# Moving the last third of a mixer's output projection into the next layer's tiles

## The chip, the cores and the metric

One core of a Trainium2 chip. The metric is the device time of one execution in microseconds (us), median over runs. Before the change it is 3393.17 us (three runs, 3390.63 to 3396.44).

## The reference

An encoder block over a sample of 1024 tokens and a prompt of 512 tokens, 1024 features, in fp32. Each of three layers has the same frame: normalise, compute, normalise the result, add it to the input.

```python
def rmsnorm(x, g):
    return x * lax.rsqrt(jnp.mean(x * x, axis=-1, keepdims=True) + NORM_EPS) * g
def swiglu(h, w1, w3, w2):
    return (jax.nn.silu(h @ w1) * (h @ w3)) @ w2
```

The order is: a half-step feed-forward (`ffn1`, hidden width 2816), the mixer (an input projection, a hyena long convolution on half of the channels, a two-way retention on the other half, an output projection with `w_out`, 1024 by 1024), and a second half-step feed-forward (`ffn2`). "Layer 1" below is `ffn1`, "layer 2" is `ffn2`.

## The kernel before, in words

**Layout.** Features lie on the 128 partitions and tokens along the columns, 1536 of them (1024 of the sample, then 512 of the prompt). An fp32 product is made of three TensorE passes: every operand is split in a high part (`hi_act`, L59, a copy on ScalarE) and a low part (`lo`, L62, a subtraction on VectorE or GpSimd), and `mm3` issues high-high (L67), high-low (L68) and low-high (L69). So a weight tile needs a load, a copy and a subtraction before its matmuls.

**Feed-forward.** `ffn` (L424) takes the columns in two halves, g = 0 (columns 0 to 767) and g = 1 (768 to 1535). Its up products (`up_unit`, tiles `ua`, `ub`, `uc`, 128x384) work on seven combinations of quarter blocks, `b11`, `b21`, `b22`, `t1` to `t4`, which `operands` (L241) builds and splits from the normalised input `xq` (`normed`, L215 to 233, which multiplies by the row of reciprocal norms `rq`). `down` (L336) makes the second product (tile `dn`), `post_quads` (L399) closes it: sums of squares (`ss`, L205), reciprocal roots (`rstd`, L86 to 100, one of its steps, L95, on GpSimd), spread over the partitions on TensorE (`rps`, L212), multiply, add the input, store. Work for the next half runs `beside` the units, a step at a time.

**Mixer, input side.** `norm_T` (L155) loads a segment of 512 columns of layer 1's output, multiplies it by the reciprocal norms (L169) and splits it into `hh` (ScalarE) and `hl` (GpSimd, L62). Then `w_in_v` (tile `v`, weights split into `w2h` and `w2l`) and `w_in_pass` (tile `wips`) multiply it by the input weights.

**Mixer, output side.** `out_proj(g)` (L1121) takes three thirds of 512 columns. `load_y` loads and splits the mixer's result into `yh` and `yl`. `proj` (L498) walks over eight output blocks of 128 features, each 8 x 3 = 24 matmuls of 128x512 (tile `proj`); the weights are loaded at L506 and their low part is made on GpSimd. `post` (L520) collects each block: its squares on ScalarE (L531), its product with the gain on VectorE (L532), the sum of squares on VectorE (L534). After the eighth block it closes the third: column sums (`rstd_cols`, `ssc`, L126), reciprocal roots, `rps` (L130), eight products z * rps (L546), eight additions of the mixer's input `o` (L547, alternately on VectorE and GpSimd), the store to `x2`, and for thirds 0 and 1 the reciprocal norms for layer 2 (`rstd_rows`).

Layer 2's first half needs columns 0 to 767, hence the closings of thirds 0 and 1; its second half needs third 2 as well.

**Order.** Every DMA is issued by SyncE. A planner simulates the program as written and fixes one order for each engine; the engines then run in that order and wait on semaphores. Tiles come from pools with a fixed number of places: a tile waits until the place that it gets is released.

Of the kernel before, what the change touches and what calls it, by code (L numbers as in the profile page):

```python
# [15 lines left out]
D = 1024  # L16
# [30 lines left out]
class Kern:  # L47
# [55 lines left out]
    def rstd_rows(self, acc, psp, rp, tag, row, **kw):  # L103


        nc = self.nc
        hl = self.xp.tile([128, 2, 512], F32R, tag="x", name="sqs")
        hi, lo = hl[:, 0], hl[:, 1]
        self.hi_act(hi, acc)
        self.lo(nc.vector, lo, acc, hi)  # L110
        ss = psp.tile([128, 512], F32, tag="nr", name="ss")
        nc.tensor.matmul(ss, lhsT=self.ones, rhs=hi, start=True, stop=False)
        nc.tensor.matmul(ss, lhsT=self.ones, rhs=lo, start=False, stop=True)
        out = rp.tile([128, 512], F32, tag=tag, name="rrow", **kw)
        nc.scalar.activation(out[0:1], ss[0:1], AF.Copy)
        c = self.sp.tile([128, 8], F32, tag="nc", name="nc")[:, :4]
        nc.sync.dma_start(c, out[0:1].rearrange("o (p c) -> o p c", c=4))
        r = self.rstd(c, 1.0 / D)
        nc.sync.dma_start(row.rearrange("o (p c) -> (o p) c", c=4), r)

    def rstd_cols(self, acc, psp, half):

        nc = self.nc
        ss = psp.tile([128, 512], F32, tag="nr", name="ssc")[:, :4]
        for t in range(4):
            nc.tensor.matmul(ss[:, t:t + 1], lhsT=acc[:, t * 128:(t + 1) * 128], rhs=self.one, start=True, stop=True)  # L126
        r = self.rstd(ss, 1.0 / D, half)
        ps = psp.tile([128, 512], F32, tag="nr", name="rps")
        for t in range(4):
            nc.tensor.transpose(ps[:, t * 128:(t + 1) * 128], r[:, t:t + 1].broadcast_to([128, 128]), self.ident)  # L130
        return ps

# [11 lines left out]

    def add_sq(self, acc, x, out, first):

        nc = self.nc
        nc.scalar.activation(out, x, AF.Square)
        if first:
            nc.vector.tensor_tensor(acc, out[:, 0], out[:, 1], ALU.add)  # L150
        else:
            for j in range(2):
                nc.vector.tensor_tensor(acc, out[:, j], acc, ALU.add)
# [24 lines left out]

    def bank(self, name):
        return self.pm.tile([128, 512], F32, tag="mm", name=name)[:, :384]  # L180
# [60 lines left out]
    def operands(self, load, X, Y):  # L241
# [17 lines left out]
        b["t3"] = self.split(Y, h12, "t3")  # L259
        b["t1"] = self.split(Y, t1, "t1")  # L260
        b["t4"] = self.split(Y, t2, "t4")
# [162 lines left out]
    def ffn(self, n, srcs, dsts, row_in, row_out, Y, side):  # L424
# [21 lines left out]
        with pool("xq", 6, side=side) as X, pool("fs", side=side) as self.fs, pool("ft", 6, side=side) as self.ft, \  # L446
                pool("fw", 10, side=side) as self.fw, pool("fr", 5, side=side) as self.fr, pool("pm", 8, space=PSUM) as self.pm:
            h = [], []
            for th in range(2):
                for _ in ready(0, th, h[th]):  # L450
                    pass
            for _ in self.operands(lambda kh, th: h[th][kh], X, Y):
                pass

            def ahead():

                for th in range(2):
# [40 lines left out]
    def proj(self, aT, w, nk, psd, wp, rp, done, eng):  # L498


        nc = self.nc
        ah, al = aT
        nb = w.shape[2]
        for c in range(w.shape[0]):
            raw = rp.tile([128, nb, 128], F32, tag="raw", name="raw2")
            nc.sync.dma_start(raw, w[c])  # L506
            for i in range(0, nb, KD):
                wh = wp.tile([128, KD, 128], F32R, tag="w", name="w2h")
                wl = wp.tile([128, KD, 128], F32R, tag="w", name="w2l")
                self.hi_act(wh, raw[:, i:i + KD])  # L510
                self.lo(eng[(i // KD + c) % len(eng)], wl, raw[:, i:i + KD], wh)
                for j in range(KD):
                    m, k = divmod(c * nb + i + j, nk)
                    if k == 0:
                        ps = psd.tile([128, 512], F32, tag="mm", name="proj")
                    self.mm3(ps, wh[:, j], wl[:, j], ah[k], al[k], k == 0, k == nk - 1)
                    if k == nk - 1:
                        done(m, ps)

    def post(self, src, dst, g, gi, zp, psp, row):  # L520
# [3 lines left out]
        z = []  # L524
        acc = zp.tile([128, 512], F32, tag="pacc", name="pacc", bufs=1)

        def done(m, ps):
            if m % 2 == 0:
                z.append(zp.tile([128, 2, 512], F32, tag=f"z{m}", name="z", bufs=1))
# [720 lines left out]
```

## Time and profile before

| | us |
|---|---|
| median of three runs | 3393.17 |
| profiled execution | 3399.09 |
| its span | 3397.3 |
| TensorE busy in it | 3087.7 (91%) |
| VectorE busy | 2644.2 (78%) |
| ScalarE busy | 1431.3 (42%) |
| GpSimd busy | 555.3 (16%) |

The mean granted clock of TensorE is 0.959 of full speed. TensorE is the busiest engine and works in order, so its idle stretches, and stretches at a lower clock, are what a change of order can win or lose. In the timeline a row is: start, duration, engine, line, operation, tile written <- tiles read, shapes, count, and in brackets the idle time of that engine just before with what ended it.

### The profile page before, as it was taken

To read this page: it belongs to the slowest core of one execution; us is meant where nothing else is said; L and a number is where in the kernel's file an instruction comes from. 1 tells how busy PE (TensorE), PEld (TensorE's weight loads), DVE (VectorE), ACT (ScalarE), POOL (GpSimd) and SP (SyncE) were. 2 spreads that over 40 slices of the span, in tenths; PEclk is the share of its full clock that TensorE was granted. 3 is DMA by queue.
4 is the path that set the end of the run, shared out by engine and by line. 5 is a ranking of instruction groups with operands and counts; after the bars stand their busy time and mean duration, and the time that the engine had idled before them with its cause. 6 is when DMAs were issued, how large, how long until landed. Compare 5 with 4: busy or idle time off the path is not lost. (4 is left out here: it accounts for less than half of the span.)

```text
span 3397.3 us, 46267 instructions
## 1 busy us (share of the span) xinstructions
PE 3087.7 (91%) x16792; PEld 2885.7 (85%) x16792; DVE 2644.2 (78%) x4316; ACT 1431.3 (42%) x2373; POOL 555.3 (16%) x400
## 2 busy tenths in 40 slices
PE   5999998999897799989897998984899999999996
PEld 4999998999897677767676887763899999999996
DVE  8788788777877599678655878886888788877776
ACT  4333464333444234355543344332433455333453
POOL 0000000000200323365322544552000000000000
PEclk8999999999998899999998999997999999999998
DMA  3567454322344534453453125454377544422343
GB/s 128 211 232 286 123 156 143 84 72 75 103 131 139 169 117 160 150 172 112 120 173 128 44 83 172 153 172 139 127 266 272 190 147 134 143 72 72 87 128 131
DMA packets 218806, 485.34 MB, mean 143 GB/s; under 512 B 36432, under 2 KB 64464, under 8 KB 216400
## 3 DMA queue, kind: packets, MB, share of 16 engines
q1 hardware_dynamic: 218576, 482.37, 43.3%
q8 instruction: 132, 2.16, 0.3%
q14 instruction: 98, 0.80, 0.1%
HBM read 382.60 MB, written 99.65 MB: 142 GB/s over the span
## 5 line engine op out<-in xcount | busy, mean ns | idle before, releaser
L68 PE MATMUL dn<-xl,w2h 128*128 128x384 f32 x1232 | 414.8, 337 | 12.7 <-DVE xl L62 12.7
L59 ACT ACTIVATE wh<-raw 128x512 fp32r<-128x512 f32 (+1 forms) x312 | 216.6, 694 | 446.0 <-PE ua L68 96.4
L59 ACT ACTIVATE wh<-s 128x512 fp32r<-128x512 f32 x352 | 221.7, 631 | 427.7 <-PE ua L68 122.3
L69 PE MATMUL dn<-xh,w2l 128*128 128x384 f32 x1232 | 392.4, 337 | 0.0
L67 PE MATMUL dn<-xh,w2h 128*128 128x384 f32 x1232 | 386.8, 337 | 1.7 <-ACT xh L59 1.6
L59 ACT ACTIVATE w2h<-raw 128x512 fp32r<-128x512 f32 (+1 forms) x348 | 236.6, 682 | 342.4 <-PE dn L68 214.9
L62 DVE TENSOR_TENSOR wl<-s,wh 128x512 fp32r<-128x512 f32 x352 | 241.8, 688 | 168.5 <-PE ub L68 84.2
L95 POOL TENSOR_TENSOR r<-m,mhalf 128x3 f32<-128x3 f32 (+1 forms) x35 | 38.8, 1108 | 1847.8 <-DVE m L94 1846.9
L62 DVE TENSOR_TENSOR w2l<-raw,w2h 128x512 fp32r<-128x512 f32 (+1 forms) x316 | 219.5, 705 | 126.0 <-ACT w2h L59 107.7
L67 PE MATMUL wips<-hh,wh 128*128 128x512 f32 x576 | 231.9, 403 | 17.7 <-ACT wh L59 16.7
L68 PEld LDWEIGHTS dn<-xl,w2h 128*128 128x128 f32 x1232 | 232.5, 189 | 15.3 <-DVE xl L62 15.3
L67 PEld LDWEIGHTS dn<-xh,w2h 128*128 128x128 f32 x1232 | 229.5, 189 | 3.8 <-ACT xh L59 3.3
L69 PE MATMUL wips<-hh,wl 128*128 128x512 f32 x576 | 230.7, 401 | 1.8 <-POOL wl L62 1.2
L68 PE MATMUL wips<-hl,wh 128*128 128x512 f32 x576 | 230.8, 401 | 0.0
L69 PEld LDWEIGHTS dn<-xh,w2l 128*128 128x128 f32 x1232 | 230.5, 189 | 0.0
L62 DVE TENSOR_TENSOR wl<-raw,wh 128x512 fp32r<-128x512 f32 (+1 forms) x276 | 199.0, 721 | 39.9 <-ACT wh L59 37.9
L67 PE MATMUL fw<-th,mh 128*128 128x256 f32 x448 | 132.3, 297 | 30.9 <-DVE spec L839 18.2
L67 PEld LDWEIGHTS wips<-hh,wh 128*128 128x128 f32 x576 | 110.4, 192 | 46.3 <-ACT wh L59 17.6
L67 PE MATMUL ua<-b11h,wh 128*128 128x384 f32 x352 | 123.7, 351 | 26.6 <-ACT b11h L59 26.6
L69 PEld LDWEIGHTS wips<-hh,wl 128*128 128x128 f32 x576 | 110.3, 192 | 30.0 <-POOL wl L62 2.4
L68 PE MATMUL fw<-tl,mh 128*128 128x256 f32 x448 | 132.3, 296 | 1.3 <-DVE tl L62 1.2
L69 PE MATMUL fw<-th,ml 128*128 128x256 f32 x448 | 130.1, 291 | 3.8 <-POOL ml L62 3.0
(342 smaller groups left out, 9088.9 us busy)
## 6 DMA issues: line engine op xcount, KB each, us to landing
raw<-ffn_w SPq DMA_DIRECT2D x440, 256.0 KB, 2.7
raw<-ws SPq DMA_DIRECT2D x220, 256.0 KB, 2.6
wsum<-ffn_w SPq DMA_DIRECT2D x60, 768.0 KB, 7.5
raw<-w_in_f SPq DMA_DIRECT2D x48, 512.0 KB, 4.3
ws<-wsum SPq DMA_DIRECT2D x30, 768.0 KB, 4.2
xq<-x SPq DMA_DIRECT2D x16, 768.0 KB, 7.2
res<-x SPq DMA_DIRECT2D x16, 768.0 KB, 6.3
raw<-w_out SPq DMA_DIRECT2D x24, 512.0 KB, 3.4
```

The costliest lines, as they stand in the source:

```text
L59: self.nc.scalar.activation(hi, src, AF.Copy)
L62: eng.tensor_tensor(lo, src, hi.bitcast(F32), ALU.subtract)
L67: mm(ps, lhsT=ah, rhs=bh, start=first, stop=False, **kw)
L68: mm(ps, lhsT=ah, rhs=bl, start=False, stop=False, **kw)
L69: mm(ps, lhsT=al, rhs=bh, start=False, stop=last, **kw)
L95: nc.gpsimd.tensor_tensor(r, m, self.mhalf[:, :n], ALU.pow)
```

## The change

- The output projection's loop (`proj`) becomes a generator that yields after each output block; `collect` takes the blocks off PSUM with two ScalarE operations (square, and copy times gain) instead of one of ScalarE and one of VectorE.
- The closing (`post`) becomes a generator with stages: reciprocal root; multiply, add, squares and store; reciprocal norm of the result. All its additions run on VectorE. The stages of closing 0 run after blocks 0, 1 and 6 of third 1; closing 1 follows third 1. The norm's row for layer 2 comes from four 128x1 matmuls and goes to DRAM without the round trip that `rstd_rows` made.
- Third 2 is no longer an `out_proj`. `last_third` runs inside `ffn2`, in tiles of that layer's pools: `y` in the operand tiles, the weights in `fr` (raw tiles, five places) and `fw`, the weight's low parts on VectorE. In the program's text it stands after the normalisation of layer 2's first half and two steps of `operands`. Its closing runs beside the units of that half.
- The pools of `xq` operands, `fw` and `fr` are opened outside of `ffn`, in both layers. In layer 1 the mixer's input tiles thus get places that `fw` and `fr` held (the pools came in another order before).

```diff
-    def proj(self, aT, w, nk, psd, wp, rp, done, eng):
+    def proj(self, aT, w, psd, wp, rp, done, eng):
...
+        for m in range(w.shape[0]):
...
+            for k in range(KD):
+                self.mm3(ps, wh[:, k], wl[:, k], ah[k], al[k], k == 0, k == KD - 1)
+            done(m, ps)
+            yield
...
             nc.scalar.activation(sq, ps, AF.Square)
-            nc.vector.tensor_scalar(z[-1][:, m % 2], ps, self.gains[:, gi, m:m + 1], None, ALU.mult)
+            nc.scalar.activation(z[m], ps, AF.Copy, scale=self.gains[:, gi, m:m + 1])
...
+    def post(self, src, dst, g, z, zp, new, old, row):
+        f = self.factor(z[KD], new)
+        next(f)
+        yield
+        r = next(f)
+        for i in range(4):
+            o = old()
...
+            for j in range(2):
+                m = 2 * i + j
+                nc.vector.tensor_tensor(z[m], z[m], r, ALU.mult)
+                nc.vector.tensor_tensor(o[:, j], z[m], o[:, j], ALU.add)
...
+    def last_third(self, g, d, src, dst, tiles):
...
+        for m in range(KD):
+            ps = self.new("proj")
+            for i in range(2):
+                w = self.fr.tile([128, 512], F32, tag="raw", name="raw3").rearrange("p (k c) -> p k c", c=128)
+                nc.sync.dma_start(w, self.io["w_out"][m][:, 4 * i:4 * i + 4])
+                wh = self.fw.tile([128, 4, 128], F32R, tag="w", name="w3h")
+                wl = self.fw.tile([128, 4, 128], F32R, tag="w", name="w3l")
+                self.hi_act(wh, w)
+                self.lo(nc.vector, wl, w, wh)
...
+            sq = self.fr.tile([128, 512], F32, tag="raw", name="sq3") if m else z[KD]
+            nc.scalar.activation(sq, ps, AF.Square)
+            nc.scalar.activation(z[m], ps, AF.Copy, scale=self.gains[:, 3, m:m + 1])
+            if m:
+                nc.vector.tensor_tensor(z[KD], sq, z[KD], ALU.add)
+            yield
+        yield from self.post(src, dst, g, z, None, lambda: self.new("nr"), self.old, None)
...
-                self.xp, zp, hpA, wp, rp = (e(pool(n, b, side="right")) for n, b in
-                                            (("xin", 2), ("zo", 1), ("hpA", 1), ("w", 4), ("raw", 2)))
+                zp, xp, hpA, wp, rp = (e(pool(n, b, side="right")) for n, b in
+                                       (("zo", 1), ("xin", 2), ("hpA", 1), ("w", 4), ("raw", 2)))
...
-                    out_proj(1, hpA, rp, wp, zp, psd, psn)
-            out_proj(2, hpA, rp, wp, zp, psd, psn)
-        with pool("yq", 20) as Y:
-            self.ffn(2, x2, outs, row2, None, Y, "left")
+                    rest = closing(0, z, zp, psn, xp)
+                    z = {}
+                    for m, _ in enumerate(out_proj(1, hpA, rp, wp, zp, psd, z)):
+                        if m in (0, 1, 6):
+                            next(rest, None)
+                    for _ in closing(1, z, zp, psn, xp):
+                        pass
+        with pool("xq", 6) as X, pool("fr", 5) as self.fr, pool("fw", 10) as self.fw, pool("yq", 20) as Y:
...
+                third = self.last_third(2, d, x1, x2, tiles)
+                for _ in ready(0):
+                    pass
+                for _ in ready(1):
+                    pass
+                ops = operands()
+                next(ops)
+                next(ops)
+                for _ in range(KD):
+                    next(third)
+                for _ in ops:
+                    pass
+                yield "units"
+                yield from third
+
+            self.ffn(2, x2, outs, row2, None, X, Y, "left", lead)
```

**Where the order moves: TensorE between the projection and layer 2.** Before, the last rows of third 2 (`proj`), its closing (`ssc`, `rps`) and the first up product:

```order
L68 MATMUL proj<-yl,w2h 128x512
L69 MATMUL proj<-yh,w2l 128x512
L126 MATMUL ssc<-ones,pacc 128x1 x4
L130 MATMUL rps<-ident,r 128x128 x4
L67 MATMUL ua<-b11h,wh 128x384
```

Now, at the same place, the last rows of third 1, the closing of third 1 (`nr`: column sums, spread, and the column sums of its result `acc`), and the first matmul of `last_third`, whose operands `y_...` are the split mixer result:

```order
L68 MATMUL proj<-yl,w2h 128x512
L69 MATMUL proj<-yh,w2l 128x512
L508 MATMUL nr<-ones,z 128x1 x4
L513 MATMUL nr<-ident,r 128x128 x4
L544 MATMUL nr<-ones,acc_21429 128x1 x4
L67 MATMUL proj<-y_21555,w3h 128x512
L68 MATMUL proj<-y_21558,w3h 128x512
```

All 192 matmuls of third 2 now stand behind the three `nr` steps of closing 1; the first `ua` follows them.

**VectorE beside the moved third.** Now, for some of its blocks: the normalisation of layer 2 (`xq`), operand splits and differences over 1536 columns (`b11l`, `t_...`, `t2l`), low parts of the third's weights (`w3l`) and sums of its squares (`y_21563`, L575):

```order
L196 SCALAR_TENSOR_TENSOR xq<-xq,gains,rq 128x384 x8
L213 TENSOR_TENSOR t_21596<-xq 128x1536
L62 TENSOR_TENSOR w3l<-raw_21718,w3h 128x512
L62 TENSOR_TENSOR w3l<-raw_21736,w3h 128x512
L216 TENSOR_TENSOR t_21598<-xq,t_21596 128x1536
L218 TENSOR_TENSOR xq<-xq 128x1536
L62 TENSOR_TENSOR t2l<-t_21598,t2h 128x1536
L575 TENSOR_TENSOR y_21563<-sq_21713,y_21563 128x512
L222 TENSOR_TENSOR t_21598<-xq,t_21598 128x1536
L575 TENSOR_TENSOR y_21563<-sq_21754,y_21563 128x512
L62 TENSOR_TENSOR w3l<-raw_21759,w3h 128x512
L62 TENSOR_TENSOR w3l<-raw_21777,w3h 128x512
```

Before, the same operand work stood among the weight splits of the first up units, with no matmul of a third beside it.

**GpSimd between layer 1 and the mixer.** Before, with the eight `hl` of the first segment ahead of three closings' roots (L95) and the weights of `w_in_v`:

```order
L62 TENSOR_TENSOR hl<-x,hh 128x512 x8
L95 TENSOR_TENSOR r<-m,mhalf 128x3 x3
L62 TENSOR_TENSOR w2l<-raw_10662,w2h 128x1024
L62 TENSOR_TENSOR w2l<-raw_10733,w2h 128x1024
L62 TENSOR_TENSOR w2l<-raw_10807,w2h 128x1024
L944 MEMSET lscale 128x1
L62 TENSOR_TENSOR w2l<-raw_10837,w2h 128x1024
L95 TENSOR_TENSOR r<-m,mhalf 128x3
```

Now:

```order
L62 TENSOR_TENSOR w2l<-raw_10662,w2h 128x1024
L62 TENSOR_TENSOR w2l<-raw_10733,w2h 128x1024
L62 TENSOR_TENSOR hl<-x,hh 128x512 x4
L62 TENSOR_TENSOR w2l<-raw_10807,w2h 128x1024
L62 TENSOR_TENSOR hl<-x,hh 128x512
L95 TENSOR_TENSOR r<-m,mhalf 128x3
L62 TENSOR_TENSOR hl<-x,hh 128x512 x3
L62 TENSOR_TENSOR w2l<-raw_10837,w2h 128x1024
L95 TENSOR_TENSOR r<-m,mhalf 128x3
```

The eight `hl`, and with them their loads on SyncE, their products on VectorE (L169) and their copies on ScalarE, moved from the start of layer 1's last `down` to its end, among the weights of `w_in_v`; layer 1's last closing has roots behind them.

## Rows read from the trace of the kernel before

**Rows 1.** The page: busy time, then TensorE's share and clock in 40 slices.
```profile
PE 3087.7 (91%) x16792; PEld 2885.7 (85%) x16792; DVE 2644.2 (78%) x4316; ACT 1431.3 (42%) x2373; POOL 555.3 (16%) x400
...
PE   5999998999897799989897998984899999999996
...
PEclk8999999999998899999998999997999999999998
```
**Rows 2.** Windows: PE, PEld, DVE, ACT, POOL busy; clock, DMA share, GB/s.
```profile
1072.00:1137.00 65.00, 29.66 (x118) 23.78 (x119) 39.84 (x62) 16.04 (x15) 17.57 (x12) 0.72 0.69 185
2323.00:2357.00 34.00, 3.23 (x14) 2.50 (x12) 15.86 (x30) 3.67 (x5) 6.94 (x5) 0.54 0.61 208
2357.00:2380.00 23.00, 9.87 (x27) 8.31 (x28) 23.00 (x27) 8.34 (x10) 0.00 (x0) 0.57 0.13 34
2420.00:2440.00 20.00, 20.00 (x118) 20.00 (x117) 13.20 (x24) 7.88 (x14) 0.00 (x0) 1.00 0.32 106
```
**Rows 3.** Timeline of PE, end of third 2 to the up units of layer 2.
```profile
2322.92 0.39 PE L69 MATMUL proj<-yh,w2l 128*128 128x512 f32 x1
2325.52 1.84 PE L126 MATMUL ssc<-ones,pacc 128*128 128x1 f32 x8 [2.21 <-DVE pacc L534]
2357.24 0.69 PE L67 MATMUL ua<-b11h,wh 128*128 128x384 f32 x1 [26.57 <-ACT b11h L59]
2365.55 0.69 PE L68 MATMUL ua<-b11l,wh 128*128 128x384 f32 x1 [7.62 <-DVE b11l L62]
2410.43 1.17 PE L205 MATMUL ss<-ones,acc 128*128 128x1 f32 x6 [4.91 <-DVE acc L195]
2450.51 0.51 PE L212 MATMUL rps<-ident,r 128*128 128x128 f32 x3 [3.45 <-DVE r L100]
```
**Rows 4.** Timeline of PE, two matmuls 24 apart at the end of third 1.
```profile
2261.65 0.39 PE L69 MATMUL proj<-yh,w2l 128*128 128x512 f32 x1
...
2267.09 0.39 PE L69 MATMUL proj<-yh,w2l 128*128 128x512 f32 x1
```
**Rows 5.** Timeline of DVE, closing of third 2 and the norm of layer 2.
```profile
2330.71 4.87 DVE L546 TENSOR_TENSOR z<-z,rps 128x512 f32<-128x512 f32 x8 [1.27 <-PE rps L130]
...
2343.25 0.69 DVE L547 TENSOR_TENSOR z<-z,o 128x512 f32<-128x512 f32 x1 [6.47 <-DMA o<-x]
...
2363.75 1.75 DVE L62 TENSOR_TENSOR b11l<-xq,b11h 128x1536 fp32r<-128x1536 f32 x1
```
**Rows 6.** The page: groups of weight splits, and the median time of weight loads to landing.
```profile
L59 ACT ACTIVATE w2h<-raw 128x512 fp32r<-128x512 f32 (+1 forms) x348 | 236.6, 682 | 342.4 <-PE dn L68 214.9
...
L62 DVE TENSOR_TENSOR w2l<-raw,w2h 128x512 fp32r<-128x512 f32 (+1 forms) x316 | 219.5, 705 | 126.0 <-ACT w2h L59 107.7
...
raw<-ffn_w SPq DMA_DIRECT2D x440, 256.0 KB, 2.7
```
**Rows 7.** Timeline of PE, waits in thirds 1 and 2.
```profile
2220.03 1.09 PE L130 MATMUL rps<-ident,r 128*128 128x128 f32 x4 [3.26 <-DVE r L100]
...
2233.87 0.58 PE L67 MATMUL b<-mh,yh 128*128 128x256 f32 x1 [4.08 <-DVE E L910]
```
**Rows 8.** Timeline of PE, last unit and last `down` of layer 1, then of layer 2.
```profile
889.89 0.41 PE L67 MATMUL ub<-t4h,wh 128*128 128x384 f32 x1 [2.51 <-DVE u L302]
...
1056.65 0.45 PE L68 MATMUL dn<-xl,w2h 128*128 128x384 f32 x1 [1.47 <-DVE xl L62]
...
3202.53 0.41 PE L67 MATMUL ub<-t4h,wh 128*128 128x384 f32 x1 [0.74 <-DVE u L302]
...
3356.59 0.45 PE L68 MATMUL dn<-xl,w2h 128*128 128x384 f32 x1 [1.47 <-DVE xl L62]
```
**Rows 9.** Timeline of PE and POOL, layer 1's end to the mixer's input projection.
```profile
1136.75 0.79 PE L67 MATMUL wips<-hh,wh 128*128 128x512 f32 x1 [16.01 <-ACT wh L59]
...
1089.73 4.65 POOL L62 TENSOR_TENSOR w2l<-raw,w2h 128x1024 fp32r<-128x1024 f32 x2 [0.16 <-ACT w2h L59]
...
1128.54 4.66 POOL L62 TENSOR_TENSOR hl<-x,hh 128x512 fp32r<-128x512 f32 x3 [16.14 <-ACT hh L59]
```

More of the change, by code (lines that the diff above doesn't have):

```diff
@@ L101, in rstd @@
         return r
[L103 to L131, printed above, removed]
     def pieces(self, t, quads, g, i):
@@ L143, in pieces @@
             a += n
[L145 to L153, printed above, removed]
     def norm_T(self, src, g, gi, hp, row, eng=None):
@@ L239, in split, with operands @@
         return h, l
-    def operands(self, load, X, Y):
+    def operands(self, load, X, Y, Z=None):
         tt = self.nc.vector.tensor_tensor
@@ L444, in ready @@
             return self.normed([srcs[g][kh][th] for kh in range(2)], pre, Y, row, xs)
-        with pool("xq", 6, side=side) as X, pool("fs", side=side) as self.fs, pool("ft", 6, side=side) as self.ft, \
-                pool("fw", 10, side=side) as self.fw, pool("fr", 5, side=side) as self.fr, pool("pm", 8, space=PSUM) as self.pm:
+        with pool("fs", side=side) as self.fs, pool("ft", 6, side=side) as self.ft, pool("pm", 8, space=PSUM) as self.pm:
             h = [], []
-            for th in range(2):
-                for _ in ready(0, th, h[th]):
-                    pass
-            for _ in self.operands(lambda kh, th: h[th][kh], X, Y):
-                pass
+            if lead is None:
+                for th in range(2):
+                    for _ in ready(0, th, h[th]):
+                        pass
+                for _ in self.operands(lambda kh, th: h[th][kh], X, Y):
+                    pass
+                lead = iter(())
+            else:
+                lead = lead(lambda i: ready(0, i, h[i]), lambda: self.operands(lambda kh, th: h[th][kh], Y, Y, X), X, Y)
+                for step in lead:
+                    if step == "units":
+                        break
             def ahead():
+                yield from lead
                 for th in range(2):
@@ L552, in done, with factor @@
-            if row is not None:
-                self.rstd_rows(a2, psp, self.xp, "x", row[:, 512 * g:512 * g + 512], bufs=2)
-        return done
+                nc.vector.tensor_tensor(z[KD], sq, z[KD], ALU.add)
+        return done
+    def factor(self, acc, new):
+        nc = self.nc
+        ss = new()[:, :4]
+        for t in range(4):
+            nc.tensor.matmul(ss[:, t:t + 1], lhsT=acc[:, t * 128:(t + 1) * 128], rhs=self.one, start=True, stop=True)
+        r = self.rstd(ss, 1.0 / D)
+        yield
+        ps = new()
+        for t in range(4):
+            nc.tensor.transpose(ps[:, t * 128:(t + 1) * 128], r[:, t:t + 1].broadcast_to([128, 128]), self.ident)
+        yield ps
@@ new lines, in post @@
+    def post(self, src, dst, g, z, zp, new, old, row):
+        nc = self.nc
+        f = self.factor(z[KD], new)
+        next(f)
+        yield
+        r = next(f)
+        a2 = None if row is None else zp.tile([128, 512], F32, tag="acc2", name="acc2", bufs=1)
+        for i in range(4):
+            o = old()
+            for part, q in self.pieces(o, src, g, i):
+                nc.sync.dma_start(part, q)
+            for j in range(2):
+                m = 2 * i + j
+                nc.vector.tensor_tensor(z[m], z[m], r, ALU.mult)
+                nc.vector.tensor_tensor(o[:, j], z[m], o[:, j], ALU.add)
+                if row is not None:
+                    sq = a2 if m == 0 else z[m]
+                    nc.scalar.activation(sq, o[:, j], AF.Square)
+                    if m:
+                        nc.vector.tensor_tensor(a2, sq, a2, ALU.add)
+            for part, q in self.pieces(o, dst, g, i):
+                nc.sync.dma_start(q, part)
+        yield
+        if row is not None:
+            ss = new()[:, :4]
+            for t in range(4):
+                nc.tensor.matmul(ss[:, t:t + 1], lhsT=a2[:, t * 128:(t + 1) * 128], rhs=self.one, start=True, stop=True)
+            r = self.rstd(ss, 1.0 / D)
+            nc.sync.dma_start(row[:, 512 * g:512 * g + 512].rearrange("o (c p) -> (o p) c", p=128), r)
```

99 lines of the change are left out of this document (49 added, 50 removed).

## The prediction

> **What bounds the kernel now.** I read the page first: TensorE is busy for 91% of the span, VectorE for 78% [rows 1]. The line of 40 slices shows where TensorE is not full: the first slice, the tenth to thirteenth (the mixer's input side), and the 28th, which covers 2293 to 2378 us and is the way from the output projection to layer 2. Its clock digit is 7 there. The windows over that way come next [rows 2]: from 2323 to 2357 TensorE works 3.2 us of 34, from 2357 to 2380 it works 9.9 of 23, both at about 0.55 of the full clock, that is near the lower level of 1.2 GHz; from 2420 on it is full at clock 1.00, 118 matmuls of 128x384 in 20 us, 0.1695 us each. The timeline of TensorE says why [rows 3]: third 2 ends at 2323.3, its closing's two steps wait for VectorE, and the first up product waits 26.57 us for `b11h`, then 7.62 for `b11l`. That wait is a chain: z * rps, 4.87 us for eight, additions that wait 6.47 for `o` [rows 5], stores, layer 2's norm, the split of `b11` at 1.75 us. No matmul is ready beside it. So 2267 to 2400 is a stretch in which VectorE and DMA set the end, while nearly everywhere else TensorE does.
>
> **The change part by part.** The sum is made against the profiled execution, 3399.1 us, which is 5.9 above the median 3393.2; the forecast of the median is 5.9 less than the sum. A measurement can tell about 0.2% from no change, 6.8 us.
>
> *Layer 1's last down.* The eight `x`, `hh` and `hl` of the mixer's first segment leave it. Layer 2 has the same down without such a guest, so it is the price list: from the last wait in the units to the same late wait in the down it takes 1056.65 - 889.89 = 166.76 us in layer 1 and 3356.59 - 3202.53 = 154.06 in layer 2 [rows 8], 12.7 us apart, and the wait in front is 2.51 against 0.74. All of it gone is 14.5 us. The bounds are 0 (the guest was not the reason) and -14.5; I take **-13**, since the rest of the two stretches is the same program.
>
> *The handover to the mixer.* What left the down arrives here, on four queues. On GpSimd the order now puts eight `hl` among four `w2l`, ahead of layer 1's last reciprocal roots. A `w2l` takes 2.33 us and an `hl` 1.55 [rows 9], so eight `hl` are 12.4 us ahead of roots that waited for none of them before; the loads of `x`, four pairs on SyncE, now stand between the weights of `v` and the stores of layer 1, at some 3 us more, the time of a load [rows 6]. In 1072 to 1137 TensorE has 29.7 us of work in 65 [rows 2], and `wips` waits 16.01 at its end [rows 9]: the chain last closing, then loads of constants, then `w_in_f` sets that end, so the 12.4 + 3 land on it whole. I take **+15**. The least is +5, if the `v` matmuls and the roots pass each other well (TensorE has 35 idle us there); the most is +22, if the products and copies of the eight also stand in line, 8 x 0.9 us, an estimate from 0.6 for a product [rows 5] and half of the 0.68 of a copy twice as wide [rows 6].
>
> *Thirds 0 and 1.* The product with the gain leaves VectorE for ScalarE, eight times 0.6 us a third, and the closing of third 0 runs in stages, so that TensorE no longer stands before its `rps`. The waits to win are 3.26 and 4.08 us [rows 7]. The additions that GpSimd did are VectorE's now, four more of 0.6 us, which takes some back. I take **-4**, bounds -9 and +3. A row of ScalarE's copy off PSUM costs nothing that ends a wait: it is busy for 42% [rows 1].
>
> *From third 1 to the full units.* Before: from 2267.1, where third 1's matmuls end [rows 4], to the start that units at full rate would have had. The `rps` at 2450.51 stands behind 336 up matmuls; 2450.5 - 336 x 0.1695 = 2393.6 [rows 2, 3]. That is 126.5 us with third 2 in it. After, by the order, TensorE stands through closing 1 with nothing else, then has 192 third matmuls, then the units:
> - closing 1 bare: by third 2's closing before, 2330.7 - 2323.3 = 7.4 us to the first product [rows 3, 5]; then products, additions and sums of squares, 24 on VectorE at 0.6 = 14.6; last column sums 2; the inputs `o`, two places as before, 6.47 again [rows 5]: 30;
> - 192 matmuls at (2267.09 - 2261.65) / 24 = 0.2267 us [rows 4]: 43.5, and 2 for a start at the low clock;
> - waits inside it: operand work of 1.75 us a piece [rows 5] stands between the weights' low parts on VectorE, four pieces before the third block's and three before the first `ua`: 10.5;
> - the first weights of the units 1.5, the waits at the second tiles' norms 6 (before 4.91 and 3.45, now spread over more matmuls [rows 3]), closing 2 beside the units 3 (sixteen operations of 0.6 in a VectorE that has 6.8 of 20 us free there [rows 2]).
>
> That is 96.5, and **-30**. The least gain is -15, if the third's blocks lose another 2 us each; the most is -40, if `o` comes in time and half of the waits hide. What goes is the bare 26.57: the operands are made beside the third. What is late next is closing 1 itself: it was hidden by third 2 before and is bare now, which is why not all of 34 + 23 us comes back.
>
> On the clock the row shows 0.54 and 0.57 on both sides of the long wait [rows 2]. The Trainium skill (TensorE: Matmul & The Clock Gate, HAM oscillation — how this bites in real kernels) says that pauses between groups of matmuls bring the engine back to its low clock each time. That rule speaks against the change. Taken for every block of the third it would make a rival, which is worked out from rows below; the row agrees for the long pause, and no row of before shows it for pauses of 1 to 3 us.
>
> Sum: -13 + 15 - 4 - 30 = **-32**, 3367 in a profiled execution, 3361 as a median.
>
> **The rivals.**
>
> *The third starves (slower).* Its weights go through five places of `fr` with 2 KB each, three to a block: two halves of the weights and the square. The second half of block m + 2 gets the place of block m's square. From the end of block m that chain is square 0.6, sum 0.6, load 2.7, copy 0.7, low part 0.7 [rows 6], 5.3 us, and there are 5.4 + 2.7 before TensorE needs it: a slack of 2.8. Two operand pieces of 1.75 in VectorE's queue and a load that lands 2 us later use it up. Each block then loses 2 to 3 us, 8 x 3 = 24, and a TensorE that pauses at each block may stay at the low level, 24 matmuls in 10.9 us in place of 5.4, 8 x 5.4 = 43. The third then costs 24 + 43 in place of 10.5 + 2, 54 more than in my sum, and the change is slower by 22: 3415. It decides from the point at which a block takes over 43.5 + 12.5 + 32 = 88 us / 8 = 11 us. For it: VectorE is busy all of 2357 to 2380 [rows 2] with this very operand work. Against it: only the blocks with operand work beside them have long queues, and from the fourth block on these pieces stand singly in the order. Chance 0.11.
>
> *Half of it, and the guest pays nothing back.* Layer 1's down gains nothing, since VectorE and not the guest held it there, and the handover pays 20: with -4 and -30 the sum is -14, 3379. For it: the wait behind the units, 1.47, is the same in both layers [rows 8]. Against: the same stretch of layer 2 is 12.7 shorter. Chance 0.15.
>
> *The gain stays out.* The third does not do what it is moved for: the closing in front of it, bare, takes as long as the wait that it removes. If closing 1 takes 40 us with its stores and inputs one after another on one queue, and the third's waits are 25, the transition is 43.5 + 40 + 25 + 12.5 = 121, -5; with the other terms the total is within 5 us of before: 3390. For it: the order puts all 192 matmuls behind the last `nr` of closing 1. Against: third 2's closing took 34 us to the first up product before with a store, a row and a norm behind it that are not in front of the third now. Chance 0.08.
>
> **How the numbers follow.** My forecast has 0.66: **3361**, its own range 3345 to 3376 by the bounds of its terms (the ends do not meet all at once). The half case ends at 3379, mostly faster by over 6.8 us (3386.4); the case without gain lies within 0.2%, the starving third above. Faster 0.66 + 0.13 = 0.79, same 0.02 + 0.08 = 0.10, slower 0.11. The range that leaves out no more than 2 in 10 reaches from 3341, where the down gives all and the transition 40, to 3392, which takes in the half case and most of the case without gain; the starving third is left out.
>
> **What the profile after would show.** Right: the wait before the first up product falls from 26.57 us to a few; `proj` matmuls at L67 of `last_third` follow a wait of 25 to 35 us for an `nr`; the late units of layer 1's down have the short waits of layer 2; `wips` starts 75 to 82 us after the last `dn` (65 before); the third takes 50 to 60 us. Wrong: waits of PE for `w3l` before most blocks with a clock near 0.5 over the whole third (starved); a down of layer 1 as long as before; a wait for closing 1 beyond 35 us.

## The result: 33 us slower, and where they went

| | before | after |
|---|---|---|
| median, us | 3394.79 (4 runs, 3390.63 to 3396.44) | 3428.08 (4 runs, 3424.40 to 3434.24) |
| profiled execution, its span | 3399.09, 3397.3 | 3428.59, 3426.4 |

The ratio is 1.0102, interval 1.0084 to 1.0120. The prediction was 3361, range 3341 to 3392. The two profiled executions lie 29.5 us apart, and the stretches below are theirs. The page of after, with TensorE's share and clock in 40 slices [rows 1]:

```profile
PE 3104.1 (91%) x16804; PEld 2898.9 (85%) x16804; DVE 2631.9 (77%) x4315; ACT 1447.9 (42%) x2409; POOL 517.3 (15%) x380
...
PE   5999999999997599998897998867989999999996
...
PEclk9999999999999799999998999988999999999998
```

TensorE's share is the same. The bad slices are the 13th and 14th (the handover to the mixer) and now two, the 27th and 28th, on the way to layer 2. TensorE's timeline gives the places at which both programs can be compared; each entry is a start in us, and the last column how much later after is:

| | before | after | later |
|---|---|---|---|
| last matmul of layer 1 | 1071.6 | 1068.7 | -2.9 |
| first `wips` of the mixer | 1136.8 | 1152.8 | 16.0 |
| last matmul of third 1 | 2267.1 | 2280.9 | 13.8 |
| first up product of layer 2 | 2357.2 | 2392.4 | 35.1 |
| last `ua<-b11h` matmul (L67) of layer 2's units | 3189.0 | 3217.7 | 28.7 |

So two stretches lose: the handover 18.9 us, the way from third 1 to the last unit 14.9. Layer 1 gains only 2.9 where its down alone was to give 13.

**Layer 1 and the handover.** The timeline of TensorE in after, at the places of [rows 8, 9]:

```profile
897.00 0.41 PE L67 MATMUL ub<-t4h,wh 128*128 128x384 f32 x1 [0.74 <-DVE u L266]
...
1053.69 0.45 PE L68 MATMUL dn<-xl,w2h 128*128 128x384 f32 x1 [1.34 <-DVE xl L62]
...
1152.76 0.79 PE L67 MATMUL wips<-hh,wh 128*128 128x512 f32 x1 [25.30 <-ACT wh L59]
```

From the first to the second row it is 156.69 us, 10.1 less than the 166.76 of before, and the wait ahead is 0.74 instead of 2.51: the guest's price is paid back. But the first row stands 7.1 us later than in before, in a part of the program in which TensorE takes the same instructions in the same order. The windows of both in mid-layer show why; the columns are the window, its length, PE busy and its count, PEld, DVE, ACT, POOL, clock, DMA share, GB/s.

```profile
700.00:800.00 100.00, 100.00 (x570) 100.00 (x569) 69.14 (x121) 38.29 (x68) 0.00 (x0) 1.00 0.26 71
```

Before:

```profile
700.00:800.00 100.00, 100.00 (x579) 100.00 (x578) 70.91 (x124) 38.77 (x70) 0.00 (x0) 1.00 0.25 74
```

TensorE is full and at full clock in both, yet after it issues 570 matmuls and before 579: 0.1754 us each in place of 0.1727.

**The way to layer 2.** Windows of after over closing 1, the whole third, and its third, fourth, fifth and seventh blocks:

```profile
2281.00:2312.00 31.00, 4.36 (x20) 3.64 (x18) 19.36 (x37) 8.50 (x14) 1.01 (x1) 0.58 0.50 143
2312.58:2388.82 76.24, 55.35 (x193) 40.88 (x193) 36.24 (x48) 22.95 (x32) 1.01 (x1) 0.84 0.30 94
...
2331.40:2344.00 12.60, 8.35 (x24) 5.89 (x24) 12.60 (x14) 3.79 (x6) 0.00 (x0) 0.63 0.08 24
2345.70:2351.90 6.20, 6.02 (x24) 4.35 (x24) 1.29 (x2) 0.56 (x3) 0.00 (x0) 1.00 0.25 85
2355.00:2364.20 9.20, 8.54 (x24) 6.05 (x24) 4.10 (x4) 1.84 (x2) 0.00 (x0) 0.66 0.10 37
2373.70:2381.40 7.70, 7.60 (x24) 5.49 (x24) 1.29 (x2) 0.54 (x2) 0.00 (x0) 0.78 0.24 68
```

TensorE's waits there, the answer to [rows 3]:

```profile
2286.73 1.83 PE L508 MATMUL nr<-ones,z 128*128 128x1 f32 x8 [5.41 <-DVE z L499]
2290.80 1.09 PE L513 MATMUL nr<-ident,r 128*128 128x128 f32 x4 [2.23 <-DVE r L100]
2310.89 1.84 PE L544 MATMUL nr<-ones,acc 128*128 128x1 f32 x8 [19.00 <-DVE acc L537]
2312.58 0.77 PE L67 MATMUL proj<-y,w3h 128*128 128x512 f32 x1
...
2331.48 0.80 PE L67 MATMUL proj<-y,w3h 128*128 128x512 f32 x1 [5.72 <-ACT w3h L59]
2336.86 0.79 PE L69 MATMUL proj<-y,w3l 128*128 128x512 f32 x1 [4.16 <-DVE w3l L62]
2345.77 0.50 PE L67 MATMUL proj<-y,w3h 128*128 128x512 f32 x1 [1.78 <-ACT w3h L59]
2355.01 0.80 PE L67 MATMUL proj<-y,w3h 128*128 128x512 f32 x1 [3.22 <-ACT w3h L59]
...
2383.15 0.50 PE L67 MATMUL proj<-y,w3h 128*128 128x512 f32 x1 [1.78 <-ACT w3h L59]
2392.36 0.69 PE L67 MATMUL ua<-b11h,wh 128*128 128x384 f32 x1 [3.15 <-ACT wh L59]
...
2492.92 0.69 PE L67 MATMUL ua<-b21h,wh 128*128 128x384 f32 x1 [7.00 <-ACT p L255]
```

The wait of 26.57 us before the first up product is gone, as forecast. In its place the third runs from 2312.58 to 2388.82, 76.2 us for 192 matmuls that take 43.5 at full rate, and waits for its weights at six of its eight blocks: TensorE is idle for 20.9 us of it, and its matmuls take 55.35. ScalarE and SyncE in after show where the weights were; the last row is a sum of SyncE's waits over the third (total, times, longest):

```profile
2282.62 2.64 ACT L59 ACTIVATE w3h<-raw 128x512 fp32r<-128x512 f32 x4 [2.66 <-DMA raw<-w_out]
...
2330.80 1.29 ACT L59 ACTIVATE w3h<-raw 128x512 fp32r<-128x512 f32 x2 [4.41 <-DMA raw<-w_out]
...
2364.23 0.60 ACT L572 ACTIVATE sq<-proj 128x512 f32<-128x512 f32 x1 [7.39 <-PE proj L69]
2364.73 0.68 ACT L573 ACTIVATE y<-proj,gains 128x512 f32<-128x512 f32 x1
2365.30 1.15 ACT L59 ACTIVATE w3h<-raw 128x512 fp32r<-128x512 f32 x2
...
2314.83 0.37 SPq L546 DMA_DIRECT2D row<-r  x1
2325.10 0.32 SPq L191 DMA_DIRECT2D rq<-row  x1
2325.47 1.37 SPq L563 DMA_DIRECT2D raw<-w_out  x3
...
2353.24 0.33 SPq L563 DMA_DIRECT2D raw<-w_out  x1
...
SPq L563 <- DVE y L575: 25.2, 5, 6.1
```

Three things are to be read there. The `w3h` of the first two blocks are done by 2285.3, but TensorE comes to them at 2312.6, since the three `nr` of closing 1 stand ahead of them in its queue. SyncE stands 10 us at the load of the norm's row (`rq`), with the third block's weight loads behind it: they go out at 2325.47, and the copies at 2330.80 wait 4.41 us for them. And from the fourth block on, ScalarE makes a block's `w3h` only after it has squared the block before (`sq`), which waits for that block's last matmul: 7.39 us idle, and the two copies go at once, so their loads had landed.

The five places of `fr` do hold loads back: 25.2 us of SyncE's waits are for the sums that free them. They do not hold the copies. The sixth block's second load goes out at 2353.24, a load lands after 2.6 us here (the median of these twelve), and its copy starts at 2365.8. From the fourth block to the eighth, the loads go out 8 to 13 us ahead of their copies.

Of TensorE's 20.9 idle us, then, 9.9 stand at the third block (5.72 and 4.16), behind SyncE and the norm that the row feeds, and 11.0 at the next five, nearly all for `w3h`.

### The profile page after: what moved, and what is told of

It reads as the page before. It is cut to its first block, busy times and chain, and to the rows that moved or that the text cites. A ratio compares the mean times of both kernels' runs of the same rounds, so it can differ in the third digit from the quotient of the medians.

```text
span 3426.4 us, 46290 instructions
## 1 busy us (share of the span) xinstructions
PE 3104.1 (91%) x16804; PEld 2898.9 (85%) x16804; DVE 2631.9 (77%) x4315; ACT 1447.9 (42%) x2409; POOL 517.3 (15%) x380
## 5 line engine op out<-in xcount | busy, mean ns | idle before, releaser
L67 PE MATMUL dn<-xh,w2h 128*128 128x384 f32 x1232 | 390.2, 337 | 1.5 <-ACT xh L59 1.5
L59 ACT ACTIVATE w2h<-raw 128x512 fp32r<-128x512 f32 (+1 forms) x340 | 228.7, 675 | 344.3 <-PE dn L68 213.0
L95 POOL TENSOR_TENSOR r<-m,mhalf 128x3 f32<-128x3 f32 (+1 forms) x35 | 37.0, 1056 | 2184.6 <-DVE m L94 2183.7
L67 PE MATMUL wips<-hh,wh 128*128 128x512 f32 x576 | 232.8, 404 | 27.7 <-ACT wh L59 26.6
L67 PEld LDWEIGHTS dn<-xh,w2h 128*128 128x128 f32 x1232 | 228.7, 188 | 3.3 <-ACT xh L59 2.8
L67 PE MATMUL fw<-th,mh 128*128 128x256 f32 x448 | 132.2, 297 | 32.2 <-DVE spec L862 18.3
L67 PEld LDWEIGHTS wips<-hh,wh 128*128 128x128 f32 x576 | 110.8, 192 | 56.3 <-ACT wh L59 27.2
L67 PE MATMUL ua<-b21h,wh 128*128 128x384 f32 x352 | 120.2, 341 | 15.5 <-ACT p L255 14.8
L68 PEld LDWEIGHTS wips<-hl,wh 128*128 128x128 f32 x576 | 110.8, 192 | 26.6
```

The lines of the kernel that those rows point to most:

```text
L59: self.nc.scalar.activation(hi, src, AF.Copy)
L67: mm(ps, lhsT=ah, rhs=bh, start=first, stop=False, **kw)
L68: mm(ps, lhsT=ah, rhs=bl, start=False, stop=False, **kw)
L95: nc.gpsimd.tensor_tensor(r, m, self.mhalf[:, :n], ALU.pow)
```

## The experiments

My theory after this reading had three causes: layer 1's pools, the order in the queues around the third, and something that slows layer 1's matmuls. The rivals: the five places of `fr` starve the third, and the staged closing or the other pools lose the time. A kernel named e is compared with after (3428.1 us) unless it says otherwise; before's median beside them was 3396.4 (e1 to e4), 3396.7 (e5 to e8) and 3395.0 (e9 to e12), beside after 3394.8, so some 2 us of a difference to after mean nothing.

**e1, layer 1's pools as before** (in `ffn`, in their old order):

```diff
...
-                with pool("xq", 6, side="right") as X, pool("fw", 10, side="right") as self.fw, pool("fr", 5, side="right") as self.fr:
-                    self.ffn(1, xs, x1, None, row1, X, Y, "right")
+                self.ffn(1, xs, x1, None, row1, None, Y, "right")
```

> The changed kernel with one thing undone: layer 1's pools are opened inside ffn again, in the order of before. Theory (the order of the pools moved the mixer's first eight x, hh and hl from layer 1's last down to the handover, and slowed layer 1's matmuls): all of the 16.0 us by which the input projection starts late comes back, 3412 us, with 578 matmuls in 100 us of layer 1 instead of 570, a last down some 14 us longer and a handover some 19 shorter. Rival (the slower matmuls come from the tiles of yq, which lie 192 bytes lower in both kernels, not from the pools' order): 570 matmuls stay, only 14 against 19 is exchanged, 3421 to 3425 us.

Measured: 3419.1 us (four runs, 3417.8 to 3420.3), 9 less. `wips` starts at 1143.0, 9.8 earlier; it stands 62.3 us behind the last `dn` (84.0 in after), and that `dn` starts 12.0 later. TensorE still issues 571 in 100 us. So it is the rival, 2 us below its range: down and handover are exchanged. The pools are one cause, and not that of the slow matmuls.

**e2, the kernel before with the changed order of layer 1's pools:**

```diff
-        with pool("xq", 6, side=side) as X, pool("fs", side=side) as self.fs, pool("ft", 6, side=side) as self.ft, \
-                pool("fw", 10, side=side) as self.fw, pool("fr", 5, side=side) as self.fr, pool("pm", 8, space=PSUM) as self.pm:
+        with ExitStack() as own:
+            X = own.enter_context(pool("xq", 6, side=side))
+            for name, bufs in (("fw", 10), ("fr", 5), ("fs", 1), ("ft", 6)) if n == 1 else (("fs", 1), ("ft", 6), ("fw", 10), ("fr", 5)):
...
```

> The kernel before with one thing done: layer 1's pools in the changed kernel's order, nothing else. Theory (the order of the pools costs what layer 1 and the handover lost): 3395 + 16 = 3411 us, the input projection starts near 1153 us, 570 matmuls in 100 us. Rival (yq's place sets the rate): 578 matmuls stay, down -14, handover +19, 3400 us.

Measured: 3407.6, ratio to before 1.0041 (1.0024 to 1.0058), 11 us more; 579 matmuls in 100 us, as the rival had it, at a time between the two expectations. Layer 1 ends 15.7 us earlier than before and the handover is 17.7 longer, so `wips` is 2.0 late. Another 5 us go between there and layer 2. What loses those stays open: from the first `wips` to the first `proj`, profiles of kernels with the same order on TensorE differ by up to 6 us (984.3 in e3, 990.7 in e11).

**e3, third 2 as a third `out_proj` again,** with the stages of closing 1 beside its blocks:

```diff
-                    for _ in closing(1, z, zp, psn, xp):
-                        pass
+                    rest = closing(1, z, zp, psn, xp)
+                z = {}
+                for m, _ in enumerate(out_proj(2, hpA, rp, wp, zp, psd, z)):
+                    if m in (0, 1, 6):
+                        next(rest, None)
+                for _ in closing(2, z, zp, psn, xp):
+                    pass
...
-            self.ffn(2, x2, outs, row2, None, X, Y, "left", lead)
+            self.ffn(2, x2, outs, row2, None, X, Y, "left")
```

> The changed kernel with the last third done as a third out_proj again (staged closings, ScalarE evictions and the changed pools kept). Theory (what the transition lost came from the third standing behind closing 1 on TensorE): closing 1 is hidden beside third 2 again, no gain and no loss of more than 5 us in the transition against before; with the 14 us that were lost up to the end of third 1 the time is 3405 to 3413 us. Rival (the staged closing with all additions on VectorE, or layer 2's pools, lost it): as slow as the changed kernel, 3422 us or more.

Measured: 3414.8, 1.8 above the range but 13 below after. `wips` is 15.7 us later than in before and layer 2's last `ua` 12.8: from there on e3 loses nothing. The staged closing and layer 2's pools are not what cost; the moved third is.

**e4, four blocks of the third between the stages of closing 1.** Operand and weight pools of layer 2 are opened while closing 1's are still there, and PSUM for all eight blocks; the norm of the second tiles follows the fifth block, and weights are split a block ahead from there on:

```diff
...
+            self.third_y(2, d, yh, yl)
+            ps = []
+            for m in range(4):
+                ps.append(self.third_mm(self.third_w(m), yh, yl))
+                if m in (0, 1, 4 - 1):
+                    next(close1, None)
...
```

> The changed kernel with four blocks of the last third written between the stages of closing 1, the norm of the second tiles behind the fifth block, and each block's weights split ahead of the block before being taken off. Theory (order on TensorE, SyncE and ScalarE, not the places of fr, kept the third late): its first matmul starts within 6 us of third 1's end instead of 31, the third ends before 2350 us instead of 2389, and the time falls by 30 to 50 us, 3380 to 3398 us. Rival (five places of fr bound the third): its blocks still take 9 us or more each, and the time stays above 3410 us.

Measured: 3397.6 (ten runs), ratio to before 1.0010 (0.9997 to 1.0022), 30 less than after. TensorE's timeline in e4:

```profile
2280.02 0.50 PE L67 MATMUL proj<-y,w3h 128*128 128x512 f32 x1 [2.13 <-ACT w3h L59]
2293.58 0.62 PE L515 MATMUL nr<-ident,r 128*128 128x128 f32 x4 [1.16 <-DVE r L100]
2314.44 1.87 PE L546 MATMUL nr<-ones,acc 128*128 128x1 f32 x8 [9.33 <-DVE acc L539]
...
2355.00 0.69 PE L67 MATMUL ua<-b11h,wh 128*128 128x384 f32 x1 [4.70 <-ACT wh L59]
```

The third starts 2.5 us behind third 1 and ends at 2349.9; the first up product comes 37 us earlier than in after. Queue order was the matter, though e4 can't say which queue.

**e5, yq at its old address.** The removed `rstd_rows` took a tag of six tiles of 32 bytes from the pool in front, so `yq` starts 192 bytes lower, at 18752 instead of 18944. e5 fills the gap:

```diff
         self.sp = e(self.pool("stats", 6))
+        self.pad = e(self.pool("pad")).tile([128, 48], F32, name="pad")
+        nc.gpsimd.memset(self.pad, 0.0)
```

> The changed kernel with 192 unused bytes behind the small tiles, so that the tiles of yq start at the address that they have in the kernel before; the rest is the changed kernel. Theory (the place of yq sets how fast layer 1's 128x384 matmuls issue): 578 of them in 100 us again instead of 570, the end of layer 1 some 9 us earlier, 3419 us. Rival (something else of the change slows them): 570 stay, 3428 us.

Measured: 3417.0 (3409.1 to 3418.3), 11 less; layer 1's last `dn` starts 11.6 us earlier. The same window in e5:

```profile
700.00:800.00 100.00, 100.00 (x579) 100.00 (x578) 71.75 (x125) 38.56 (x70) 0.00 (x0) 1.00 0.25 74
```

**e6, the row's load behind four blocks' weight loads** (the norm of the second tiles written behind these blocks, its loads queued after the last of their weights):

```diff
...
-                for _ in ready(1):
-                    pass
+                for _ in range(4):
+                    next(third)
+                with self.tc.issue_after(self.load3.ins):
+                    for _ in ready(1):
+                        pass
...
```

> The changed kernel with the norm of the second tiles written behind four blocks of the last third, its loads queued on SyncE behind those blocks' weight loads. Theory (SyncE stood 10 us at the load of the row, with the third's weights behind it): the wait of 5.72 us before the third's third block and the 4.16 behind it are gone, the third ends 8 to 15 us earlier, 3412 to 3420 us. Rival (the norm that comes later makes the first up product wait as much longer): the third ends earlier, but the wait before ua grows by the same, 3425 us or more.

Measured: 3422.3 (3419.1 to 3424.4), 6 less. The waits of 5.72 and 4.16 are gone, and two later blocks wait longer in their place:

```profile
2342.16 0.80 PE L67 MATMUL proj<-y,w3h 128*128 128x512 f32 x1 [3.15 <-ACT w3h L59]
...
2356.74 0.79 PE L67 MATMUL proj<-y,w3h 128*128 128x512 f32 x1 [3.61 <-ACT w3h L59]
```

The third still takes 73.5 us, and the time lies between the two expectations. Alone, SyncE was a small part.

**e7, weights ahead, nothing else:**

```diff
...
         for m in range(KD):
             ps = self.new("proj")
+            if m == 0:
+                ws = weights(0)
+            now, ws = ws, weights(m + 1) if m + 1 < KD else None
             for i in range(2):
+                wh, wl = now[i]
```

> The changed kernel with the high and low parts of a block's weights written ahead of the square and the copy that take the block before off PSUM, nothing else. Theory (on ScalarE w3h of the next block stood behind the square, which waits for the last matmul of this one): the five waits of 1.78 us at the blocks are gone and with them blocks at a low clock, 9 to 15 us, 3413 to 3419 us. Rival (five places of fr, or SyncE behind the row, keep the weights late): the waits stay or move, 3424 to 3430 us.

Measured: 3401.9 (ten runs, 3397.9 to 3408.3), 26 less, more than theory had. Its window over the third, TensorE's only waits from closing 1 to the first up product, and ScalarE between two blocks:

```profile
2305.00:2359.00 54.00, 49.25 (x194) 39.48 (x194) 35.15 (x47) 22.50 (x31) 1.01 (x1) 0.88 0.39 123
```

```profile
2303.53 1.84 PE L544 MATMUL nr<-ones,acc 128*128 128x1 f32 x8 [18.94 <-DVE acc L537]
2305.23 0.77 PE L67 MATMUL proj<-y,w3h 128*128 128x512 f32 x1
...
2329.92 0.80 PE L69 MATMUL proj<-y,w3l 128*128 128x512 f32 x1 [4.65 <-DVE w3l L62]
2362.48 0.69 PE L67 MATMUL ua<-b11h,wh 128*128 128x384 f32 x1 [3.15 <-ACT wh L59]
...
2344.00 0.63 ACT L59 ACTIVATE w3h<-raw 128x512 fp32r<-128x512 f32 x1
2345.24 0.63 ACT L59 ACTIVATE w3h<-raw 128x512 fp32r<-128x512 f32 x1 [0.61 <-DMA raw<-w_out]
2348.93 0.60 ACT L582 ACTIVATE sq<-proj 128x512 f32<-128x512 f32 x1 [3.06 <-PE proj L69]
```

The third takes 53.7 us in place of 76.2, with `sq3` still in the ring of five places: TensorE is idle for 4.8 us of it (20.9 in after), and its slower matmuls cost 5.5 (11.8 in after; both are the busy time less 43.5). So with the pauses went half of what the low clock cost.

The edit moves more than ScalarE's copies. Six of the third's weight loads now go out before the norm's row (four in after), VectorE's low parts come earlier, and in the ring a load waits for an earlier square. e6 took SyncE's wait away alone and the third stayed at 73.5 us, and in after the loads of the last five blocks had landed well before their copies. These two and e7 together point to ScalarE's order as the main cause, but no run moved the copies alone.

Of the 26 us, the profile has 22 behind the end of third 1. The rest lies in the mixer, which took 1121.3 us from `wips` to that end (1128.2 in after).

**e8, everything together,** with six blocks beside closing 1:

> Everything together: six blocks of the last third beside closing 1, the norm of the second tiles behind the sixth, weights ahead, layer 1's pools as before the change, yq at its old address. Theory (the three causes add): from e4's 3398 us, less 9 for yq's address, less 9 for layer 1's pools, less 5 to 10 for two more blocks in closing 1's wait: 3370 to 3378 us. Rival (the six blocks delay closing 1, and the norm behind it becomes the wait before ua): 3380 us or more, with a wait of over 10 us before the first up product.

Measured: 3375.0 (five runs, 3373.6 to 3375.8), ratio to before 0.9933 (0.9921 to 0.9946): it beats both kernels. The rival's wait is there but smaller than said:

```profile
2305.46 0.79 PE L67 MATMUL proj<-y,w3h 128*128 128x512 f32 x1 [8.64 <-ACT w3h L59]
...
2329.68 0.69 PE L67 MATMUL ua<-b11h,wh 128*128 128x384 f32 x1 [8.92 <-ACT wh L59]
...
2437.44 0.69 PE L67 MATMUL ua<-b21h,wh 128*128 128x384 f32 x1 [6.57 <-ACT p L257]
```

**e9, e7 and e1 and e5 in one, third behind closing 1 as changed:**

> The changed kernel with the three side costs mended and the third left where the change put it, behind closing 1: weights ahead (e7), layer 1's pools as before (e1), yq at its old address (e5). Theory (they add, -26, -9 and -11 of 3428): 3380 to 3386 us, faster than before by 10 to 16; that is what the move of the third is worth alone. Rival (they overlap, the norm row still stands in SyncE): 3390 us or more.

Measured: 3380.9, ratio to before 0.9955 (0.9942 to 0.9969). The three add as expected. What is left of the change is a gain of 14 us. Hiding closing 1 (e8) would be worth 6 to 8 more (3380.9 - 3375.0, or 21.7 against 14.1 under the before of each), but the intervals of the two ratios overlap, so this is not clear of noise.

**e10, the kernel before with yq 192 bytes lower:**

```diff
-        c = self.sp.tile([128, 8], F32, tag="nc", name="nc")[:, :4]
+        c = self.sp.tile([128, 8], F32, tag="m", name="nc")[:, :4]
```

> The kernel before with yq 192 bytes lower, by a small tile that shares its places with another; nothing else. Theory (the address alone slows layer 1's matmuls): 570 matmuls in 100 us of layer 1, layer 1's end 9 to 12 us later, 3404 to 3408 us. Rival (the address matters only beside the changed kernel's other tiles): 578, 3396 us.

Measured: 3405.6, ratio 1.0043 (1.0026 to 1.0059), 10.6 us more, layer 1's last `dn` 11.3 later:

```profile
700.00:800.00 100.00, 100.00 (x570) 100.00 (x569) 69.11 (x120) 38.58 (x69) 0.00 (x0) 1.00 0.25 72
```

**e11, 64 bytes in place of 192** (`[128, 16]` in e5's tile):

> The changed kernel with 64 unused bytes in place of e5's 192: yq starts at 18816, a multiple of 128 and not of 512. If what counts is a start at a multiple of 128 bytes, 578 matmuls in 100 us as in e5; if it is a start at a multiple of 512, 570 as in the changed kernel.

One run, 3428.6 us, 572 matmuls in 100 us. Neither expectation: a multiple of 128 is not enough. Yet 18816 is not as slow as 18752: layer 1's last `dn` starts at 1062.8, between after (1068.7) and e5 (1057.1). The last section says where.

**e12, e8 with layer 2's squares two steps later** (`for _ in range(self.lag): yield` ahead of the sum of squares):

> e8 with one thing more: in layer 2 the squares of the second half's input are written two steps later than its loads, so that ScalarE doesn't stand at them. Theory (the wait of 6.57 us for the product p on ScalarE comes from squares that wait for their input, queued ahead of it): that wait falls below 1 us and the time by 4 to 7, 3368 to 3371 us. Rival (the wait moves to the norm's sum or to the operand loads): within 2 us of e8's 3375.

Measured: 3375.0, no change. The 6.57 is gone, but a later unit waits twice as long for the same product:

```profile
2684.75 0.69 PE L68 MATMUL ua<-b21h,wh 128*128 128x384 f32 x1 [13.56 <-ACT p L260]
```

## Why the prediction was wrong

Step by step, terms of the prediction's sum against the two profiles:

| term | predicted | measured | |
|---|---|---|---|
| layer 1's last down | -13 | -11.8 (-10.1 and -1.8) | right |
| rate of layer 1's matmuls | not seen | +9 to +11 | missing (e5, e10) |
| handover | +15 | +18.9 | in its bounds; the pools' order makes it (e1), which queue holds it was not tested |
| thirds 0 and 1, with the mixer | -4 | -2.2 | near, by luck: the waits of 3.26 and 4.08 are gone, others of 3.09 and 5.74 came, and this stretch varies by 9 (1121.3 in e7, 1130.5 in e11) |
| third 1 to full units | -30 | +14.9 | failed |

**The step that failed** is the sum for the last term, 96.5 us against 141.4 (126.5 + 14.9), in two of its items. The first, closing 1 bare, 30, measured 31.6 (2280.93 to 2312.58), right.

"192 matmuls ... 43.5, and 2 for a start at the low clock" with "waits inside it ... 10.5" is 56, measured 76.2: 20 short, half of it pauses (20.9 in place of 10.5), half slow matmuls (11.8 in place of 2). I looked for waits in VectorE's queue and in the ring, had costed ScalarE at nothing by its busy share of 42%, and had no term for SyncE at the row. With the weights ahead (e7) the third takes 53.7, inside the item. An engine with 58% of its time free held the path at five blocks, because it works in order: the copy that TensorE wanted next stood behind a square that wanted TensorE's last matmul.

The last item, "first weights ... 1.5, the waits ... 6, closing 2 ... 3", so 10.5, is 33.4: 3.5 from the third's last matmul to the first up product, and from there to units at full rate 29.9 by the same reckoning (3217.7 - 3189.0 = 28.7 behind 2393.6, less 2392.4). Before had lost 36.4 there, of which I had read only the waits of [rows 3]. TensorE's waits of 0.7 to 7.0 us up to 2508, the 7.00 for `p` the longest, add up to 17.0; the clock is below full in several stretches (0.89 from 2392.4 to 2422, 0.78 from 2493 to 2512). This item is why the move, with the rest mended, is worth 14 us and not 30: in e9 closing 1 takes 26.7 and the third 53.1, both less than predicted, and the way from the first up product to full units still 29.5. e12 took one wait away and had no gain, so what bounds that stretch stays open.

**The missing step**: where pools move, addresses move. The diff removes a helper and with it 192 bytes, and layer 1 issues 1.5% slower. e5 gives the address back and gains 11 us, e10 takes it from before and loses 10.6. Nothing in the trace of before could price it.

**The rivals.** The starving third came true in its effect (blocks of 9.5 us, slower by 33; its price was 11 us a block and 3415) and not in its cause, the five places: they held loads, but no copy. "Half of it" was wrong: the guest did pay back (e2: layer 1 ends 15.7 us earlier). The bare closing was sized right, at 31.6 us, and it mattered less than I thought: e8 against e9 gives 6 to 8 us for hiding it, because the norm's row and the operands then become the wait (8.92 before `ua`, for a `wh` that ScalarE copies behind operand splits).

**Readings and sums.** Six of the prediction's do not hold, and none moves the sum by more than 4 us. The wait of 4.08 us is the mixer's convolution's (`b<-mh,yh`), not the projection's. The slices that are not full on the mixer's input side are the 13th and 14th. Seven operand pieces of 1.75 are 12.3, not 10.5. 0.68 us is no copy twice as wide but a mean of two widths; a copy of 128x512 takes 0.63, so the handover's most was +25. 0.1695 us counts matmuls at the edges of a window of 20 us; it is 0.1727 over 100, 1.1 us for 336. "The gain stays out" adds up to -7 and 3386. Of the signs, the wait for an `nr` was 19.0 us, not 25 to 35, and `wips` came 84.0 behind the last `dn`, not 75 to 82.

**The clock.** The Trainium skill (TensorE: Matmul & The Clock Gate, HAM oscillation — how this bites in real kernels) says that waits between groups of matmuls bring the engine back to its low clock, each time anew. The trace of after agrees in part: behind the waits of 5.72 us (with 4.16 inside the block) and 3.22 the blocks ran at 0.63 and 0.66, while of the four blocks behind 1.78 three ran at 1.00 and one at 0.78. So the clock did not stay low over the third, as the rival had it, and more of the loss is pauses: of 76.2 us TensorE was idle for 20.9, and its slower matmuls cost 11.8.

## What to carry to other kernels

When a block's evictions and the next block's operand splits share an engine, write the splits first; an in-order engine with a low busy share can still hold the path, so read the order in which it takes its work, not its share. Before an edit removes or reorders tiles, see which other tiles change their addresses, and measure that alone; a kernel that is slower by 1% may hold a gain of its own (here 14 us) under side costs that can each be undone.

## What was not expected of the hardware

A matmul of 128x384 issues every 0.1727 us or every 0.1754 in layer 1, with TensorE full and its granted clock 1.00 in both. What differs is the SBUF address at which `yq` begins in the built program: 18944 gives 578 or 579 in 100 us (before, e2, e5, e8, e9, e12), 18752 gives 570 or 571 (after, e1, e3, e4, e6, e7, e10), 18816 gives 572 (e11). It costs 10.6 us of the whole in one direction (e10) and 11 in the other (e5).

The matmuls that slow down most are those that read a tile of `yq`. Between 700 and 880 us of after, those on `b22`, `t1`, `t3` and `t4` follow one another at 0.1765 to 0.1767 us in the mean; those on `b11`, `b21` and `t2`, which lie in the pool `xq` and kept their place, at 0.1739 to 0.1760. In before all are at 0.1732 to 0.1749. In e11 the first are as slow (0.1765 to 0.1769), but the last down, which reads `yq` as well, runs nearly as fast as in before (290 in 50 us in both). Windows in that down of after and of e11, and in layer 2 of after:

```profile
950.00:1000.00 50.00, 50.00 (x285) 50.00 (x284) 43.57 (x78) 27.71 (x50) 0.00 (x0) 1.00 0.42 119
...
950.00:1000.00 50.00, 50.00 (x290) 50.00 (x289) 40.63 (x71) 24.72 (x43) 0.00 (x0) 1.00 0.46 132
...
3000.00:3100.00 100.00, 100.00 (x579) 100.00 (x578) 71.42 (x125) 39.10 (x70) 0.00 (x0) 1.00 0.26 74
```

In layer 2 of after the tiles of `yq` lie at other places with the same offset to 512 bytes, and the count is 579. So the address of these tiles alone does not settle it. Nor does their distance to the weights, taken to 512 bytes: in e11 it is the same for the up products and the last down, which run at different rates. What does was not found.
